# Running two experts chunk by chunk in turn, with the last pair staggered by three chunks

## The chip, the cores and the metric

The kernel is one program on one core of a Trainium2 chip. The metric is the device time of one execution in microseconds. The five engines have their own instruction streams, each executed in the order in which the program issues it: TensorE (PE, with its weight loads PEld), VectorE (DVE), ScalarE (ACT), GpSimd (POOL) and SyncE (SP, which here only issues loads).

## The reference

The reference is a two-layer decoder trunk on 256 tokens of width 1024. The change lies in the second layer's channel mixer, eight SwiGLU experts of which each token uses two:

```python
logits = (t @ router_w).astype(jnp.float32)
top_v, top_i = lax.top_k(logits, TOP_K)          # TOP_K = 2 of N_EXPERTS = 8
top_w = jax.nn.softmax(top_v, axis=-1)
gates = jnp.sum(jax.nn.one_hot(top_i, N_EXPERTS) * top_w[..., None], axis=1)
for e in range(N_EXPERTS):
    y = y + gates[:, e:e + 1] * swiglu(t, w_gate[e], w_up[e], w_down[e])
# swiglu(h, g, u, d) = (silu(h @ g) * (h @ u)) @ d, with d_ff = 3584
```

After it come a gated residual add and a final RMSNorm of each row.

## The kernel before

**The weight stream.** Every weight is float32 and is split on the chip into a high part (fp32r) and a rest. The class `Stream` does this for all weights in the order in which they are used. SP loads units of 1 MB (128 x 2048 floats) into raw buffers (line 144), ACT copies a unit to its high part `whi` (line 162), DVE subtracts to get the rest `wlo` (line 183). In the expert part there are four places for `whi` and three for `wlo`. When TensorE's program asks for unit n (`get`), the program issues `whi` of unit n+3 and `wlo` of unit n+2. Both overwrite the place of unit n-1, so they wait until TensorE has finished with that unit.

**One turn.** Each of the eight experts is cut into CH = 7 chunks of 512 hidden columns. A chunk has six units: two for gate, two for up, two for down. The program works in turns, one chunk each, with the down products one turn late. A turn for chunk (e, ch) issues, in this order:

- the gate products of the chunk into `ps_gate` (`wide`, line 1099), with the transposes of the previous chunk's activation in their middle (`turn`, line 1137, then ACT and DVE split it into `g`, lines 446 and 447)
- the up products into `ps_up` (also `wide`), with ACT's Silu of the gate bank in their middle (line 1262)
- the down products of the previous chunk, `pend`, into two banks `ps_y` (`down`, line 1159), and among them DVE's product `act * ps_up` (`product`, line 1280).

So a turn takes its gate and up products from its own chunk, and its down products from the chunk of the turn before.

**Wide and narrow experts.** Up to 128 tokens are gathered per expert. If an expert has more than 64, each pair of weight blocks needs three passes (high x high, high x rest, rest x high). If it has at most 64, the high and the low parts of its tokens stand side by side in the 128 columns and two passes do, but the two halves of the result have to be added afterwards: ACT copies the bank (`folded`, line 1111) and one product with `onto` adds it (line 951). The choice is made when the program runs. `by_width(e, wide, narrow, *sums)` writes both versions and a branch of TensorE's sequencer picks one (line 947). In a turn whose `pend` is of the same expert, the addition onto `ps_up` rides inside the narrow side of a down step's branch; otherwise it has a branch of its own, whose other side is empty (lines 1277 and 1278). With the inputs of this run experts 0, 2, 3 and 6 are wide, and 1, 4, 5 and 7 are narrow: a turn of a wide expert has 24 gate products, one of a narrow expert 16.

**Order of the experts.** They run one after another, 56 turns. The gathered tokens `xe` are made for two experts at a time, at the last turn of each odd expert. The gate and up banks come from four rotating banks "A", `ps_y` from two banks "C".

**Small work, one job a step.** A deque `jobs` gives up one entry at each `step()`. A turn has 15 steps: 7 in the gate products, 4 in the up products, 4 in the down products. When an expert is through, `finish(e)` queues seven entries (two copies `y_fold` line 1175, nothing, an addition under a branch, line 1180, nothing, then twice `y_out` line 1186 with its DMA to `y_rows` in DRAM, line 1187). Expert 7's result never goes to DRAM. For the others `bring_back` queues 22 entries after turn (7,2): four indirect gathers of `y_rows` by POOL (`gather_rows`, line 1196), six empty ones, and then four times ACT's `second` (line 1200), DVE's `first` (line 1203) and DVE's `onto_x` (lines 1207 and 1208). `second` and `first` need the gathered rows.

**The end.** After the last turn the last chunk's down products and `last_rows` follow: the scatter of expert 7's rows, the final norm and the stores.

Of the kernel before, what the change touches and what calls it, by code (L numbers as in the profile page):

```python
# [14 lines left out]
F32 = mybir.dt.float32  # L15
# [4 lines left out]
AF = mybir.ActivationFunctionType  # L20
# [3 lines left out]
P = 128  # L24
D = 1024
KD = D // P
# [7 lines left out]
E = 8  # L34
CH = 7
FC = FF // CH
NFC = FC // P
# [5 lines left out]
CAP = P  # L43

NARROW = 64


V_ADAB, V_ATTN, V_FFN, V_QN, V_KVN, V_OUT, V_FB = 0, 48, 56, 64, 66, 67, 75
# [193 lines left out]
def trunk_kernel(ctx: ExitStack, tc: tile.TileContext, x, c, positions, w_early, w_moe, router_w,  # L242
                 vecs, ada_b, final_g, consts, out):
    nc = tc.nc
# [16 lines left out]
    def bank(tag, shape, name):  # L261
        return psum.tile(shape, F32, tag=tag, name=name, bufs={"A": 4, "B": 2, "C": 2}[tag])
# [105 lines left out]
    order = early_order()  # L368
# [530 lines left out]
    def experts(l, outer, dram, ps_x, rs):  # L899
# [17 lines left out]
        w = outer.tile([P, 4, NB], F32, name="w")  # L917
# [26 lines left out]
        def by_width(e, wide, narrow, *more):  # L944


            with tc.If((held[0] & (1 << e)) == 0) as cmp:
                wide()
            with cmp.Else():
                for steps in (*more, narrow):  # L950
                    steps()  # L951

        held = []
# [26 lines left out]
        with tc.tile_pool(name="route", bufs=1, reuse_waits="tile") as pool:  # L980
# [9 lines left out]
            for c in halves:  # L990
                for b in range(NB):
                    ps = bank("B" if c.start else "A", [P, 512], "ps_h")
# [4 lines left out]
            ps = bank("A", [P, NB, P], "ps_r")  # L997
# [36 lines left out]
            picked = pick(0)  # L1034
            pk = next(picked)
# [34 lines left out]
        with tc.tile_pool(name="moe", bufs=1, reuse_waits="tile") as pool:  # L1070
# [36 lines left out]
            def folded(ps):  # L1107


                t = pool.tile([P, FC], F32R, name="fold")  # L1110
                nc.scalar.activation(t, ps, AF.Copy)  # L1111
                return partial(nc.tensor.matmul, ps, onto, t, start=False, stop=True, skip_group_check=True)

            y_ps, jobs = {}, deque()

            def step():

                job = jobs.popleft() if jobs else None
                if job is not None:
                    job()  # L1120
# [20 lines left out]
                    g += [both[:, i].rearrange("p w s -> p (w s)") for i in range(n)]  # L1141
                    yield

            def down(pend, *sums):
                e, ch, g = pend
                if ch == 0:
                    y_ps[e] = [bank("C", [P, 512], "ps_y") for _ in range(2)]
                for f in range(NFC):
                    hi, lo = ws.half()
                    both = g[f]  # L1150

                    def products(*passes):
                        first, last = ch == 0 and f == 0, ch == CH - 1 and f == NFC - 1
                        steps = [(n, hf) for n in range(len(passes)) for hf in range(2)]
                        if last:
                            steps.sort(key=lambda s: s[1])
                        for n, hf in steps:
                            part, w = passes[n]
                            nc.tensor.matmul(y_ps[e][hf], both[:, part], w[:, halves[hf]], start=(first and n == 0),  # L1159
                                             stop=(last and n == len(passes) - 1))  # L1160

                    first, second, even = slice(0, CAP), slice(CAP, 2 * CAP), slice(0, 2 * CAP, 2)
                    by_width(e, partial(products, (first, hi), (first, lo), (second, hi)),
                             partial(products, (even, hi), (even, lo)), *(sums if f == 1 else ()))
                    yield f
                    step()

# [45 lines left out]
            def last_rows(e, fg):  # L1213

                o = out.rearrange("(b p) d -> p b d", p=P)
                bt = back.pop(e)
                ts = [scratch([P, 512], F32, "yt") for _ in range(2)]
                for hf, c in enumerate(halves):
                    nc.vector.tensor_mul(ts[hf], y_ps[e][hf], rows[l, 5][:, c])
                rs = []  # L1220
                for b in range(NB):
                    ss = tiny.tile([P, 2], F32, name="ss", bufs=4)
                    for hf, c in enumerate(halves):
                        ps = bank("A", [P, 512], "ps_sc")
                        nc.tensor.matmul(ps, bt[:, b * P:(b + 1) * P], ts[hf], start=True, stop=True)  # L1225
                        xs = x_sb[:, b, c]
                        nc.vector.scalar_tensor_tensor(xs, ps, gates[:, b, e:e + 1], xs, ALU.mult, ALU.add)
                        square_sum(xs, ss[:, hf:hf + 1])
                    rs.append(row_r(ss, D, "x"))
                for b in range(NB):  # L1230
                    for c in halves:
                        t = scratch([P, 512], F32, "fin")
                        nc.vector.scalar_tensor_tensor(t, x_sb[:, b, c], rs[b], fg[:, c], ALU.mult, ALU.mult)  # L1233
                        nc.sync.dma_start(o[:, b, c], t)

            pend = None
# [3 lines left out]
            held.append(nc.tensor.value_load(bits[0:1, 0:1], min_val=0, max_val=(1 << E) - 1))  # L1240
            next(picked)
            jobs += [None, None, None, None] + puts + [gating, rows_and_shares]
            for e in range(E):
                for ch in range(CH):
                    pg = bank("A", [P, FC], "ps_gate")
                    for k in wide(e, pg):
                        if (e, ch) == (0, 0) and k % 2:
                            next(ahead, None)
                        elif k == 5 and pend is not None:
                            pend, *_ = turn(pend)  # L1250
                        else:
                            step()
                    add = folded(pg)
                    act = pool.tile([P, FC], F32, name="act")
                    if ch == CH - 2 and e % 2 and e + 1 < E:
                        picked = pick(e + 1)
                        next(picked)
                    pu = bank("A", [P, FC], "ps_up")
                    ahead = gather(e + 1, pk) if ch == CH - 1 and e % 2 and e + 1 < E else iter(())
                    for k in wide(e, pu, add):  # L1260
                        if k == 4:
                            nc.scalar.activation(act, pg, AF.Silu)
                            if (e, ch) == (E - 1, CH - 1):
                                nc.scalar.preload_act_table_set("natural_log_exp_and_others")  # L1264
                        if k % 2:
                            next(ahead, None)
                        else:
                            step()
                    parts = deque([slice(0, FC)])
                    add = folded(pu)  # L1270

                    within = pend is not None and pend[0] == e and (e, ch) != (E - 1, CH - 1)

                    def product():
                        if parts:
                            if not within:
                                with tc.If((held[0] & (1 << e)) != 0):  # L1277
                                    add()
                            c = parts.popleft()
                            nc.vector.tensor_mul(act[:, c], act[:, c], pu[:, c])  # L1280

                    new, turned_ = (e, ch, act), iter(())
                    if (e, ch) == (E - 1, CH - 1):
                        turned_ = turn(new)
                        new = next(turned_)
                        product()
                        product()
                    for f in down(pend, *((add,) if within else ())) if pend is not None else ():
                        if f >= 2:
                            next(turned_, None)  # L1290
                        if f % 2:
                            product()
                    while parts:
                        product()
                    if ch == 0 and e:
                        jobs.extend(finish(e - 1))
                    if (e, ch) == (E - 1, 2):
                        jobs.extend(bring_back())
                    if ch == CH - 2 and e % 2 and e + 1 < E:
                        pk = next(picked)  # L1300
                    pend = new
                while jobs:
                    step()
            for _ in turned_:
                pass
            fg = raw_pool.tile([P, RAW], F32, tag="raw", name="fg")[:, :D]
            nc.sync.dma_start(fg, bass.AP(tensor=final_g.tensor, offset=final_g.offset, ap=[[0, P], [1, D]]))
            for _ in down(pend):
                pass
            return last_rows(E - 1, fg)  # L1310

# [175 lines left out]
    return [w[i:i + 2] for w in (g, u, d) for i in range(0, len(w), 2)]  # L1487


def moe_order():  # L1490
    order, prev = [], []
    for e in range(E):
        for ch in range(CH):
            order += [(w, e, ch, k) for w in "gu" for k in range(KD // 2)] + prev
            prev = [("d", e, ch, f) for f in range(NFC)]
    return order + prev


# [109 lines left out]
```

## Time and profile before

| | |
|---|---|
| Median of 3 runs | 1466.74 us (1466.71 to 1466.99) |
| The profiled execution | 1467.24 us, span 1465.5 us |
| Granted TensorE clock, mean | 0.993 |
| PE / DVE / ACT busy over the span | 1381.7 / 1239.7 / 1058.2 us |
| Expert turns | 536.63 us to the end of the span |

The span runs from the first to the last instruction; the execution's time has 1.7 us around it. The useful way to read this kernel is by turns: each begins with the first gate product after a down product, and the busy time of each engine within a turn shows which of them is the limit there.

### The profile page before, as it was taken

To read this page: it belongs to the slowest core of one execution; us is meant where nothing else is said; L and a number is where in the kernel's file an instruction comes from. 1 tells how busy PE (TensorE), PEld (TensorE's weight loads), DVE (VectorE), ACT (ScalarE), POOL (GpSimd) and SP (SyncE) were. 2 spreads that over 40 slices of the span, in tenths; PEclk is the share of its full clock that TensorE was granted. 3 is DMA by queue.
4 is the path that set the end of the run, shared out by engine and by line. 5 is a ranking of instruction groups with operands and counts; after the bars stand their busy time and mean duration, and the time that the engine had idled before them with its cause. 6 is when DMAs were issued, how large, how long until landed. Compare 5 with 4: busy or idle time off the path is not lost. (4 is left out here: it accounts for less than half of the span.)

```text
span 1465.5 us, 21366 instructions
## 1 busy us (share of the span) xinstructions
PE 1381.7 (94%) x7305; PEld 1149.6 (78%) x7305; DVE 1239.7 (85%) x1177; ACT 1058.2 (72%) x1191; POOL 31.0 (2%) x42
## 2 busy tenths in 40 slices
PE   7999999999999989998999999999898999999876
PEld 7987899999899877886667887887666667887654
DVE  5987877777796469889988888888999998889997
ACT  5566644444557567778888778778989888778975
POOL 1000000000000020000000000000000000000200
PEclk9999999999999999999999999999999999999999
DMA  9974678787664229999999999999999999999993
GB/s 370 417 294 185 240 267 314 287 311 286 230 247 161 87 96 349 366 376 417 424 400 377 375 377 376 371 371 348 405 425 424 427 426 404 373 378 395 404 409 132
DMA packets 71100, 488.07 MB, mean 333 GB/s; under 512 B 8241, under 2 KB 8881, under 8 KB 13362
## 3 DMA queue, kind: packets, MB, share of 16 engines
q1 hardware_dynamic: 68178, 480.33, 83.6%
q10 hardware_dynamic: 2016, 3.67, 0.7%
q8 instruction: 96, 1.57, 0.4%
q0 software_dynamic: 768, 2.15, 0.4%
q14 instruction: 42, 0.34, 0.1%
HBM read 481.35 MB, written 4.72 MB: 332 GB/s over the span
## 5 line engine op out<-in xcount | busy, mean ns | idle before, releaser
L183 DVE TENSOR_TENSOR wlo<-raw,whi 128x2048 fp32r<-128x2048 f32 (+1 forms) x474 | 920.4, 1975 | 53.6 <-ACT whi L162 48.4
L162 ACT ACTIVATE whi<-raw 128x2048 fp32r<-128x2048 f32 (+1 forms) x474 | 764.5, 1662 | 106.9 <-PE ps_gu L396 77.4
L1099 PE MATMUL ps_gate<-whi,xe 128*128 128x512 f32 x672 | 243.6, 402 | 2.8 <-PEq L1180 2.2
L1099 PE MATMUL ps_up<-whi,xe 128*128 128x512 f32 x672 | 231.7, 391 | 0.0
L1099 PE MATMUL ps_gate<-wlo,xe 128*128 128x512 f32 x448 | 182.6, 408 | 24.4 <-DVE wlo L183 22.8
L1159 PE MATMUL ps_y<-whi,g 128*128 128x512 f32 x664 | 195.3, 393 | 1.6 <-PEq L1277 1.5
L1099 PE MATMUL ps_up<-wlo,xe 128*128 128x512 f32 x448 | 178.5, 398 | 13.8 <-DVE wlo L183 13.7
L1099 PEld LDWEIGHTS ps_gate<-whi,xe 128*128 128x128 f32 x672 | 128.5, 191 | 27.6 <-issue 4.4
L1159 PE MATMUL ps_y<-wlo,g 128*128 128x512 f32 x440 | 142.7, 403 | 5.9 <-DVE wlo L183 5.9
L1159 PEld LDWEIGHTS ps_y<-whi,g 128*128 128x128 f32 x664 | 125.9, 191 | 28.5 <-issue 2.9
L1099 PEld LDWEIGHTS ps_up<-whi,xe 128*128 128x128 f32 x672 | 127.7, 190 | 24.5
L1099 PEld LDWEIGHTS ps_gate<-wlo,xe 128*128 128x128 f32 x448 | 86.4, 193 | 59.9 <-DVE wlo L183 46.8
L395 PE MATMUL ps_gu<-dT_hi,whi 128*128 128x256 f32 x432 | 122.5, 284 | 0.0
L397 PE MATMUL ps_gu<-dT_hi,wlo 128*128 128x256 f32 x432 | 122.2, 283 | 0.0
L396 PE MATMUL ps_gu<-dT_lo,whi 128*128 128x256 f32 x432 | 122.2, 283 | 0.0
L1099 PEld LDWEIGHTS ps_up<-wlo,xe 128*128 128x128 f32 x448 | 85.6, 191 | 40.8 <-DVE wlo L183 24.1
L1159 PEld LDWEIGHTS ps_y<-wlo,g 128*128 128x128 f32 x440 | 80.7, 192 | 32.7 <-DVE wlo L183 19.2
L446 ACT ACTIVATE g<-ps_gt 128x512 fp32r<-128x512 f32 x55 | 32.9, 599 | 83.0 <-PE ps_gt L1137 83.0
L395 PEld LDWEIGHTS ps_gu<-dT_hi,whi 128*128 128x128 f32 x432 | 82.8, 192 | 1.2 <-issue 0.2
L396 PEld LDWEIGHTS ps_gu<-dT_lo,whi 128*128 128x128 f32 x432 | 82.8, 192 | 1.2 <-issue 0.2
L397 PEld LDWEIGHTS ps_gu<-dT_hi,wlo 128*128 128x128 f32 x432 | 82.8, 192 | 0.0
L330 DVE CUSTOM_DVE_ANT_0 raw<-raw,c_row,vc 128x1024 f32<-128x1024 f32 x56 | 71.1, 1279 | 0.0
(325 smaller groups left out, 1788.6 us busy)
## 6 DMA issues: line engine op xcount, KB each, us to landing
raw<-in_w_moe_dram SPq DMA_DIRECT2D x336, 1024.0 KB, 7.8
raw<-in_w_early_dram SPq DMA_DIRECT2D x114, 1024.0 KB, 7.0
y_rows<-y_out ACTq DMA_DIRECT2D x14, 256.0 KB, 8.7
raw<-in_w_early_dram SPq DMA_DIRECT2D x6, 512.0 KB, 8.6
gate<-in_ada_b_dram SPq DMA_DIRECT2D x4, 512.0 KB, 5.7
x_sb<-in_x_dram SPq DMA_DIRECT2D x1, 1024.0 KB, 7.1
out_dram<-fin SPq DMA_DIRECT2D x4, 256.0 KB, 2.0
fg<-in_final_g_dram SPq DMA_DIRECT2D x1, 512.0 KB, 6.8
```

The costliest lines, as they stand in the source:

```text
L162: self.nc.scalar.activation(hi, raw, AF.Copy)
L183: self.nc.vector.tensor_sub(parts[1], raw, parts[0].bitcast(F32))
L330: nc.vector.tensor_tensor_reduce(out=w, in0=w, in1=c_row, scale=1.0, scalar=vec(l, V_ADAB + section * KD + k, 1), op0=ALU.mult, op1=ALU.ad ...
L395: nc.tensor.matmul(out_, lh, rh, start=start, stop=False)
L396: nc.tensor.matmul(out_, lh, rl, start=False, stop=False)
L397: nc.tensor.matmul(out_, ll, rh, start=False, stop=stop)
L446: nc.scalar.activation(hi, src, AF.Copy)
L1099: nc.tensor.matmul(ps, both[:, part], w[:, halves[kk % 2]], start=(k == 0 and n == 1), stop=(k == KD - 2 and n == 2 * len(passes)))
L1159: nc.tensor.matmul(y_ps[e][hf], both[:, part], w[:, halves[hf]], start=(first and n == 0), stop=(last and n == len(passes) - 1))
```

## The change

The turns of two experts, 2i and 2i+1, alternate chunk by chunk. For the pair 6 and 7 a list `SKEW` gives the order 6 7 6 6 7 6 6 7 6 6 7 7 7 7, so that expert 6 has its last turn when expert 7 has three of its seven, and its last down products fall into the turn of 7's fourth. The weights are streamed in that order.

Each expert of a pair has two `ps_y` banks of its own, two "C" and two "A"; the other two "A" banks are one fixed `ps_gate` and one fixed `ps_up`. The chunk whose down products run in a turn is now mostly the other expert's. The addition onto `ps_up` rides inside the down step in all turns but the first and the last, and where the two experts differ it does so by a branch inside each side of the outer branch. `finish` is queued after the turn that holds an expert's last down products, and for expert 6 `bring_back` right behind it.

```diff
+SKEW = (0, 1, 0, 0, 1, 0, 0, 1, 0, 0, 1, 1, 1, 1)
...
+            pg, pu, *y_of = [bank("A", [P, 512], name) for name in ("ps_gate", "ps_up", "ps_yb", "ps_yb")]
+            y_of = [[bank("C", [P, 512], "ps_ya") for _ in range(2)], y_of]
...
-            def down(pend, *sums):
+            def down(pend, of, *sums):
...
-                    y_ps[e] = [bank("C", [P, 512], "ps_y") for _ in range(2)]
+                    y_ps[e] = y_of[e % 2]
...
-                    by_width(e, partial(products, (first, hi), (first, lo), (second, hi)),
-                             partial(products, (even, hi), (even, lo)), *(sums if f == 1 else ()))
+                    steps = (partial(products, (first, hi), (first, lo), (second, hi)),
+                             partial(products, (even, hi), (even, lo)))
+                    if f == 1 and sums and of != e:
+
+                        steps = [partial(by_width, of, x, x, *sums) for x in steps]
+                    by_width(e, *steps, *(sums if f == 1 and of == e else ()))
...
-            for e in range(E):
-                for ch in range(CH):
-                    pg = bank("A", [P, FC], "ps_gate")
...
+            for e, ch in moe_turns():
...
-                    within = pend is not None and pend[0] == e and (e, ch) != (E - 1, CH - 1)
...
+                within = pend is not None and not end
...
-                    if ch == 0 and e:
-                        jobs.extend(finish(e - 1))
-                    if (e, ch) == (E - 1, 2):
+                if pend is not None and pend[1] == CH - 1:
+                    jobs.extend(finish(pend[0]))
+                    if pend[0] == E - 2:
                         jobs.extend(bring_back())
...
+def moe_turns():
+
+
+    turns = [(e + i, ch) for e in range(0, E - 2, 2) for ch in range(CH) for i in range(2)]
+    ch = [0, 0]
+    for i in SKEW:
+        turns.append((E - 2 + i, ch[i]))
+        ch[i] += 1
+    return turns
```

## Rows read from the trace of the kernel before

**Rows 1.** The page, busy time of each engine over the whole span.
```profile
PE 1381.7 (94%) x7305; PEld 1149.6 (78%) x7305; DVE 1239.7 (85%) x1177; ACT 1058.2 (72%) x1191; POOL 31.0 (2%) x42
```

**Rows 2.** Timeline of PE at the borders of turn (7,0).
```profile
1334.57 0.62 PE L1159 MATMUL ps_y<-whi,g 128*128 128x512 f32 x2
1335.02 0.39 PE L1099 MATMUL ps_gate<-whi,xe 128*128 128x512 f32 x1
1335.26 0.39 PE L1099 MATMUL ps_gate<-wlo,xe 128*128 128x512 f32 x1
1335.49 0.39 PE L1099 MATMUL ps_gate<-whi,xe 128*128 128x512 f32 x1
...
1349.60 0.40 PE L1099 MATMUL ps_gate<-whi,xe 128*128 128x512 f32 x1
```

**Rows 3.** Windows cut at turn borders: PE, PEld, DVE, ACT, POOL, clock, DMA, GB/s.
```profile
550.89:569.39 18.50, 17.22 (x76) 13.93 (x77) 17.19 (x21) 14.35 (x12) 0.00 (x0) 1.00 0.86 324
569.39:653.42 84.03, 84.03 (x381) 69.54 (x380) 73.46 (x41) 65.53 (x51) 0.00 (x0) 1.00 0.98 371
653.42:668.00 14.58, 14.24 (x64) 11.34 (x62) 13.71 (x8) 13.37 (x11) 0.00 (x0) 1.00 1.00 400
761.30:778.08 16.78, 15.69 (x69) 12.35 (x68) 14.98 (x9) 13.54 (x12) 0.00 (x0) 1.00 0.94 343
1034.92:1107.04 72.12, 65.51 (x272) 48.11 (x270) 72.12 (x41) 64.96 (x51) 0.00 (x0) 1.00 1.01 421
1335.02:1349.60 14.58, 14.24 (x64) 11.34 (x62) 13.71 (x8) 13.37 (x11) 0.00 (x0) 1.00 1.00 410
1349.60:1365.21 15.61, 13.25 (x56) 9.65 (x54) 13.79 (x9) 13.40 (x14) 0.00 (x0) 1.00 1.00 399
1394.61:1418.05 23.44, 16.21 (x56) 11.71 (x54) 23.12 (x19) 16.20 (x15) 0.00 (x0) 0.85 1.00 404
```

**Rows 4.** Timeline of DVE over a turn of narrow expert 4.
```profile
1047.69 0.68 DVE L1280 TENSOR_TENSOR act<-act,ps_up 128x512 f32<-128x512 f32 x1
1048.28 6.69 DVE L183 TENSOR_TENSOR wlo<-raw,whi 128x2048 fp32r<-128x2048 f32 x3
1054.90 0.69 DVE L447 TENSOR_TENSOR g<-ps_gt,g 128x512 fp32r<-128x512 f32 x1
1055.51 6.69 DVE L183 TENSOR_TENSOR wlo<-raw,whi 128x2048 fp32r<-128x2048 f32 x3
1062.11 0.68 DVE L1280 TENSOR_TENSOR act<-act,ps_up 128x512 f32<-128x512 f32 x1
```

**Rows 5.** Timeline of DVE over a turn of wide expert 0.
```profile
633.25 0.69 DVE L1280 TENSOR_TENSOR act<-act,ps_up 128x512 f32<-128x512 f32 x1 [0.33 <-PE ps_y L1159]
633.86 6.70 DVE L183 TENSOR_TENSOR wlo<-raw,whi 128x2048 fp32r<-128x2048 f32 x3
641.96 0.69 DVE L447 TENSOR_TENSOR g<-ps_gt,g 128x512 fp32r<-128x512 f32 x1 [1.40 <-ACT g L446]
```

**Rows 6.** Waits from 536 us on: who waited for whom, us in total, times, longest.
```profile
PE ps_y L1159 <- PEq L1277: 1.5, 3, 0.6
...
ACT whi L162 <- DMA raw<-in_w_moe_dram: 0.8, 2, 0.5
```

**Rows 7.** Branches of line 947: duration in ns, smallest, median, largest.
```profile
L947 PEldq COMPARE_BRANCH  x1093: 66/176/372, 536.4 to 1453.0; - x183
```

**Rows 8.** Timeline of ACT: expert 6's rows leave in turn (7,1), the first `second`.
```profile
1355.71 0.60 ACT L1186 ACTIVATE y_out<-ps_y 128x512 f32<-128x512 f32 x1 [0.40 <-ACT y_out L1186]
1356.34 0.33 ACTq L1187 DMA_DIRECT2D y_rows<-y_out  x1
...
1360.81 0.59 ACT L1262 ACTIVATE act<-ps_gate 128x512 f32<-128x512 f32 x1
...
1390.16 0.72 ACT L1200 ACTIVATE got<-got,share 128x512 f32<-128x512 f32 x1
```

**Rows 9.** Timeline of POOL: the four gathers.
```profile
1366.76 2.85 POOL L1196 DMA_INDIRECT got<-y_rows,row_of  x1 [830.71 <-DVE wlo L183]
1369.92 1.75 POOL L1196 DMA_INDIRECT got<-y_rows,row_of  x1 [0.30 <-PE ps_gate L1099]
```

**Rows 10.** Tile `got`, the gathers' landing; then DMA issues, us from issue to landing.
```profile
DMA to landing us min/median/max: 10.5/13.4/15.0
...
y_rows<-y_out ACTq DMA_DIRECT2D x14, 256.0 KB, 8.7
...
gate<-in_ada_b_dram SPq DMA_DIRECT2D x4, 512.0 KB, 5.7
```

**Rows 11.** Timeline of DVE around the start of turn (7,2), then the first `first`.
```profile
1364.16 6.69 DVE L183 TENSOR_TENSOR wlo<-raw,whi 128x2048 fp32r<-128x2048 f32 x3
1370.78 0.69 DVE L447 TENSOR_TENSOR g<-ps_gt,g 128x512 fp32r<-128x512 f32 x1
...
1392.43 0.74 DVE L1203 SCALAR_TENSOR_TENSOR got<-got,share 128x512 f32<-128x512 f32 x1
```

More of the change, by code (lines that the diff above doesn't have):

```diff
@@ L1220, in last_rows @@
                 rs = []
+                free = [pg, pu, *y_of[E % 2]]
                 for b in range(NB):
@@ L1223, in last_rows @@
                     for hf, c in enumerate(halves):
-                        ps = bank("A", [P, 512], "ps_sc")
+                        ps = free.pop(0)
                         nc.tensor.matmul(ps, bt[:, b * P:(b + 1) * P], ts[hf], start=True, stop=True)
@@ L1242, in experts @@
             jobs += [None, None, None, None] + puts + [gating, rows_and_shares]
-            for e in range(E):
-                for ch in range(CH):
-                    pg = bank("A", [P, FC], "ps_gate")
[L1246 to L1270, printed above, removed]
-                    within = pend is not None and pend[0] == e and (e, ch) != (E - 1, CH - 1)
[L1274 to L1285, printed above, removed]
-                        product()
[L1287 to L1294, printed above, removed]
-                    if ch == 0 and e:
-                        jobs.extend(finish(e - 1))
-                    if (e, ch) == (E - 1, 2):
-                        jobs.extend(bring_back())
[L1299 to L1303, printed above, removed]
@@ new lines, in experts, with product @@
+            for e, ch in moe_turns():
+                end = (e, ch) == (E - 1, CH - 1)
+                for k in wide(e, pg):
+                    if (e, ch) == (0, 0) and k % 2:
+                        next(ahead, None)
+                    elif k == 5 and pend is not None:
+                        pend, *_ = turn(pend)
+                    else:
+                        step()
+                add = folded(pg)
+                act = pool.tile([P, FC], F32, name="act")
+                if ch == CH - 2 and e % 2 and e + 1 < E:
+                    picked = pick(e + 1)
+                    next(picked)
+                ahead = gather(e + 1, pk) if ch == CH - 1 and e % 2 and e + 1 < E else iter(())
+                for k in wide(e, pu, add):
+                    if k == 4:
+                        nc.scalar.activation(act, pg, AF.Silu)
+                        if end:
+                            nc.scalar.preload_act_table_set("natural_log_exp_and_others")
+                    if k % 2:
+                        next(ahead, None)
+                    else:
+                        step()
+                parts = deque([slice(0, FC)])
+                add = folded(pu)
+                within = pend is not None and not end
+                def product():
+                    if parts:
+                        if not within:
+                            with tc.If((held[0] & (1 << e)) != 0):
+                                add()
+                        c = parts.popleft()
+                        nc.vector.tensor_mul(act[:, c], act[:, c], pu[:, c])
+                new, turned_ = (e, ch, act), iter(())
+                if end:
+                    turned_ = turn(new)
+                    new = next(turned_)
+                    product()
+                    product()
+                for f in down(pend, e, *((add,) if within else ())) if pend is not None else ():
+                    if f >= 2:
+                        next(turned_, None)
+                    if f % 2:
+                        product()
+                while parts:
+                    product()
+                if pend is not None and pend[1] == CH - 1:
+                    jobs.extend(finish(pend[0]))
+                    if pend[0] == E - 2:
+                        jobs.extend(bring_back())
+                if ch == CH - 2 and e % 2 and e + 1 < E:
+                    pk = next(picked)
+                pend = new
@@ L1304, in experts @@
+            while jobs:
+                step()
             for _ in turned_:
@@ L1307, in experts @@
             nc.sync.dma_start(fg, bass.AP(tensor=final_g.tensor, offset=final_g.offset, ap=[[0, P], [1, D]]))
-            for _ in down(pend):
+            for _ in down(pend, E - 1):
                 pass
@@ L1487, in moe_units @@
     return [w[i:i + 2] for w in (g, u, d) for i in range(0, len(w), 2)]
+def moe_turns():
[5 more added lines that the diff above has]
+    return turns
 def moe_order():
     order, prev = [], []
[L1492 to L1495, printed above, removed]
+    for e, ch in moe_turns():
+        order += [(w, e, ch, k) for w in "gu" for k in range(KD // 2)] + prev
+        prev = [("d", e, ch, f) for f in range(NFC)]
     return order + prev
```

## The prediction

> **What bounds the kernel now.** I read the page first, then the borders of the turns, then the engines' busy time between borders, then the DVE stream inside a turn, and last the path of expert 6's rows. Over the whole span PE is busy 94% and DVE 85% [rows 1]; that is an average over stages and says little here. Turn borders are found on PE's timeline: turn (7,0) runs from 1335.02 to 1349.60, and inside it the products start 0.23 us apart [rows 2].
>
> I call a turn by the width of its gate and up products and then of its down products: WW, WN, NW, NN. Cut at the borders [rows 3], the expert part shows two limits. Five WW turns take 84.03 us, 16.81 each, and PE is busy in all of it. Five NN turns take 72.12 us, 14.42 each, and now DVE is busy in all of it while PE has 65.51. Two NW turns, (1,0) and (7,0), each right after a WW turn, take 14.58. The DVE stream says why 14.42 is a floor [rows 4]: three `wlo` of 1 MB units, `g`, three more `wlo`, the product, with no idle time, 1047.69 to 1062.11. That work is the same for a wide expert, only that DVE there stands between its pieces, 1.40 us before `g` for instance [rows 5]. So PE waits for DVE in narrow experts and DVE for PE in wide ones. Loads are not the limit: in the whole expert part ACT waited 0.8 us for raw weights [rows 6], and five NN turns ran at 421 GB/s [rows 3].
>
> **The change part by part, the turns.** Alternating puts WN and NW turns where WW and NN turns were, but only where a wide expert meets a narrow one: pairs 0/1 and 6/7. Pair 2/3 is wide twice and 4/5 narrow twice, so their turns stay WW and NN: nothing.
>
> NW is measured, 14.58. An undisturbed WN turn is not in the trace. It has 8 products fewer than WW, so 16.81 - 8 x 0.23 = 14.97; below, DVE's 14.42 bounds it, above, the 16.78 of turn (2,0), which is WN with the branch of line 1277 and leftovers of the gathering in it [rows 3]. I take 14.97, because PE is the limit in the WW turn that it is derived from. A WW and an NN turn, 31.23, so become a WN and an NW turn, 29.55: 1.68 saved. The floor, two DVE turns, would save 2.39; the upper end, 16.78 + 14.58, would lose 0.13.
>
> Pair 0/1 has six WW and six NN turns to convert: 6 x 1.68 = 10.1 us. In pair 6/7 the order 6 6 7 leaves a WW turn in each group of three, and the last three turns of expert 7 stay NN: three conversions, 5.0 us. Ends for the nine: -21.5 and +1.2 us.
>
> Start: the second turn, now (1,0), still carries DVE work left from routing. DVE had 17.19 us in it, and the turn took 18.50 as WW [rows 3], 1.7 over a plain one. As NW it cannot be shorter than 17.2, 2.6 over. Cost 0.9.
>
> **Branches and banks.** The addition onto `ps_up` loses its own branch. PE waited for that three times, 1.5 us in total [rows 6]; all three are in turns that lose it: -1.5. In its place comes a branch inside a branch. The existing branches take 0.176 us in the median and 0.372 at most [rows 7], on a sequencer that issues ahead of PE, and five WW turns with 13 of them each show PE without a gap [rows 3]. I take 0 (worse: third rival).
>
> One bank each for gate and up instead of rotating ones: the product that frees `ps_up` ends at 1048.4 [rows 4], before the next turn's first gate product at 1049.3, and the up products come 16 products later. The Silu that reads the gate bank is over at 1361.4 [rows 8], 3.8 us before the next turn. Cost 0. Without that cover PE would wait for the rest of a 0.7 us product.
>
> `finish` made an NN turn 15.61 instead of 14.42 [rows 3], 1.2 us. It runs seven times before and after: 0. If the second pair of y banks spares half of each, -4; a loss I exclude, its instructions are the same.
>
> **The rows of expert 6.** The work of `bring_back` costs (7,4) 23.44 - 14.42 = 9.0 us, because DVE is full there [rows 3]. It falls into an NN turn again, (7,5): no difference. What differs is how long it has been prepared. Before, `finish(6)` ran in (7,1) and the first `second` stood in ACT's stream at 1390.16 [rows 8], 23.4 us after the first gather began [rows 9]. Now expert 6 is through in the turn of (7,3), `finish` fills the gate products of (7,4), and the gathers, two empty steps short of `second`, come right behind.
>
> Put the start of (7,4) at T and use (7,1), which began at 1349.60, as its pattern:
>
> - The second DMA to `y_rows` is issued at 1356.34, T + 6.7 [rows 8].
> - POOL begins the first gather at 1366.76, when that DMA has landed, T + 17.2, and the second at 1369.92, T + 20.3 [rows 9]. `second` reads what the second gather brings.
> - A gather lands 10.5 to 15.0 us after its issue, 13.4 in the median [rows 10]: T + 30.8 to T + 33.7 with the first two.
> - Turn (7,5) begins at T + 15.6. `second` is its third step, `first` its fourth, both before the program asks for the second gate unit. DVE by then has the `wlo` of three units to do, which in (7,2) were done at 1370.85, 5.6 us into the turn [rows 11]: T + 21.2.
>
> From then on `first` heads DVE's queue and waits for `second`, and behind it stand all further `wlo`, behind these PE. With 0.72 us for `second` DVE stands from T + 21.2 to between T + 31.5 and T + 34.4: 10.3 to 13.2 us, in a stage where DVE is the limit, so all of it is lost. ACT stands too, so no `whi` is made ahead.
>
> The lower end: as soon as DVE stands no raw buffer is freed and the weight stream dries up, so the gather may finish faster. A 512 KB load took 5.7 us elsewhere [rows 10]; with that, 5.5 us are lost. Most of the gather still runs under the stream, so I take 10.5. PE idle that long will drop to the lower of its two clock levels, as (7,4) did before with 0.85 granted; DVE was busy 23.12 of those 23.44 us [rows 3], so this adds nothing.
>
> **Sum.** -10.1 - 5.0 + 0.9 - 1.5 + 10.5 = -5.2 us. Against the profiled execution, 1467.24 (span 1465.5 and 1.7 around it), that is 1462.0. The median of the runs is 0.5 below that execution, so I forecast 1461.5.
>
> **Rivals.**
>
> *The gathers are hardly late.* If puts and gathers land sooner than in (7,1), or the stream dries up early, 0 to 5.5 us are lost instead of 10.5: 1451 to 1456.5. For it: 5.7 us for a load of the same size. Against: every gather took over 10 us, and the puts 8.7 in the median [rows 10]. The Trainium skill ("DMA: Bandwidth & Descriptors", section "Anatomy of one DMA — SWDGE (gpsimd) path") puts a DMA at about 2.0 us plus its bytes at 436 GB/s. As an estimate from that page a put would take 2.6 and a gather 3.2 us, the second gather would land before T + 21.2, and the sum would be -15.7. The trace does not agree: 13.4 us in the median, with the weight stream on the same engines.
>
> *The lead is too short (slower).* DVE can be two units ahead of PE at most. In a WW turn it idles 16.81 - 14.42 = 2.4 us because it waits at `g` and at the product for PE. If in a WN turn it still idles that much, the turn takes 16.8, nothing is saved in the nine conversions, and the time is 1461.5 + 15.1 = 1476.6. It decides against the change from 2.9 + 5.2 = 8 us lost, that is 0.9 us in each of nine. For it: (2,0), 16.78. Against: NW turns with 14.58, where DVE was the one that ran through.
>
> *The inner branch drains PE (slower).* With an addition in one side only, the skipped side must still signal, and line 1277 shows what that costs when nothing else is in it: 1.5 us in three, 0.5 each [rows 6]. A turn whose own expert is wide and whose down products are the other's has such a side: 6 + 7 + 7 + 4 = 24 turns, nearly all bound by PE, 12 us: 1473.5. Against: an inner side still holds the down products, which can carry the signal, as the outer ones do now. The Trainium skill ("Runtime: NRT & Kernel Launch", section "Instruction fetch mechanics") says that a taken branch whose target lies outside the fetched window stalls for a fetch, and the doubled code makes turns longer. No branch among 1093 took over 0.372 us here.
>
> **How the numbers follow.** Forecast 0.50 (1457 to 1465, mostly the landing time); gathers hardly late 0.27; lead too short 0.10; drains 0.10; the rest 0.03. A measurement of this kernel can tell about 0.2%, 2.9 us, from no change: faster is below 1463.8, slower above 1469.7. Of the forecast four fifths lie below 1463.8; with the first rival 0.68. The rest of it and mild forms of the two slow rivals make 0.12, the slow rivals 0.20. The range of 1449 to 1471 holds the forecast, nearly all of the first rival and mild forms of the others; the likeliest one's own is 1457 to 1465.
>
> **What the profile after would show.** WN turns near 15.0 and NW turns near 14.6 in pairs 0/1 and 6/7, unchanged steady turns in 2/3 and 4/5; no wait of PE on line 1277 in expert turns except the first and last. In (7,5) ACT idle at line 1200 for a DMA of `got`, and DVE idle about 10 us at line 1203. I am wrong if that idle time is missing, if WN turns stay above 15.9, or if PE waits for its sequencer at line 947 or a new one like it in wide turns.

## The result, and the profile after

The changed kernel takes 1480.39 us (median of 4 runs, 1475.68 to 1480.68) against 1466.72; the ratio is 1.0087, 95% interval 1.0066 to 1.0108. It is slower by 13.7 us. The forecast was 1461.5 with a range up to 1471: wrong in direction and outside its range.

The profiled execution has a span of 1478.9, 13.4 over the one before. I found the borders of the turns as before and cut windows there; the columns are those of [rows 3].

```profile
552.40:571.05 18.65, 16.25 (x62) 12.45 (x63) 17.02 (x19) 14.59 (x12) 0.00 (x0) 0.91 0.85 315
664.79:679.90 15.11, 15.11 (x69) 12.49 (x68) 12.95 (x8) 10.94 (x10) 0.00 (x0) 1.00 0.99 406
679.90:696.06 16.16, 14.85 (x64) 11.13 (x62) 16.16 (x10) 15.13 (x12) 0.00 (x0) 1.00 1.00 398
815.83:832.65 16.82, 16.82 (x78) 13.91 (x77) 14.70 (x9) 13.11 (x11) 0.00 (x0) 1.00 0.98 382
1266.19:1284.23 18.04, 17.13 (x78) 13.84 (x76) 16.40 (x10) 14.82 (x12) 0.00 (x0) 1.00 0.98 383
1284.23:1298.85 14.62, 14.28 (x64) 11.26 (x63) 14.50 (x9) 13.41 (x11) 0.00 (x0) 1.00 0.99 405
1298.85:1313.93 15.08, 15.08 (x70) 12.49 (x68) 12.97 (x8) 10.97 (x10) 0.00 (x0) 1.00 1.01 419
1394.29:1409.57 15.28, 13.01 (x55) 9.65 (x54) 12.94 (x8) 13.40 (x14) 0.00 (x0) 1.00 1.00 409
1409.57:1442.74 33.17, 15.92 (x56) 11.05 (x54) 21.23 (x19) 17.46 (x16) 5.53 (x4) 0.82 0.78 289
1442.74:1478.90 36.16, 25.19 (x83) 16.66 (x81) 27.22 (x26) 17.12 (x24) 0.00 (x0) 0.83 0.17 65
```

The rows are turn (1,0); a WN and an NW turn of pair 0/1; a WW turn of pair 2/3; a WW, NW and WN turn of pair 6/7; then (7,4), (7,5), and (7,6) with the end. Two things stand out. In pair 0/1 a WN turn takes 15.11, as forecast, but the NW turn after it takes 16.16 and DVE is busy in all of it: together 31.27, no less than the 31.23 of a WW and an NN turn. And (7,5) takes 33.17.

Here is DVE in that WN turn and at the start of the NW turn, which begins at 679.90 (timeline after):

```profile
670.14 0.69 DVE L449 TENSOR_TENSOR g<-ps_gt,g 128x512 fp32r<-128x512 f32 x1 [1.43 <-ACT g L448]
670.75 2.28 DVE L185 TENSOR_TENSOR wlo<-raw,whi 128x2048 fp32r<-128x2048 f32 x1
673.40 4.49 DVE L185 TENSOR_TENSOR wlo<-raw,whi 128x2048 fp32r<-128x2048 f32 x2 [0.37 <-ACT whi L164]
677.82 0.68 DVE L1289 TENSOR_TENSOR act<-act,ps_up 128x512 f32<-128x512 f32 x1
678.86 6.70 DVE L185 TENSOR_TENSOR wlo<-raw,whi 128x2048 fp32r<-128x2048 f32 x3 [0.37 <-ACT whi L164]
```

DVE idles 1.43, 0.37 and 0.37 us; the first, at `g`, is the wait that a WW turn shows [rows 5]. It has nothing more to do by the program's order, and then has no stock when the light turn begins.

The end of the stall in (7,5), on PE, ACT and DVE (three timelines after):

```profile
1415.21 0.40 PE L1101 MATMUL ps_up<-whi,xe 128*128 128x512 f32 x1
1427.79 0.79 PE L1101 MATMUL ps_up<-wlo,xe 128*128 128x512 f32 x1 [12.19 <-DVE wlo L185]
```
```profile
1400.67 0.33 ACTq L1197 DMA_DIRECT2D y_rows<-y_out  x1
...
1424.03 0.72 ACT L1210 ACTIVATE got<-got,share 128x512 f32<-128x512 f32 x1 [12.41 <-DMA got<-y_rows,row_of]
```
```profile
1408.49 4.49 DVE L185 TENSOR_TENSOR wlo<-raw,whi 128x2048 fp32r<-128x2048 f32 x2
1424.78 0.75 DVE L1213 SCALAR_TENSOR_TENSOR got<-got,share 128x512 f32<-128x512 f32 x1 [11.80 <-ACT got L1210]
```

This is the chain that was forecast: `first` heads DVE's queue for 11.80 us because `second` waits for a gather. DVE had two units done when it began to stand, not three, and PE stopped after the first `whi` product of the first up unit.

**A correction to the section on the kernel.** It says that the program, asked for unit n, issues `whi` of n+3 and `wlo` of n+2. These rows show one unit less: with PE in the gate products of (7,5), DVE had done the two gate units and no up unit. The condition in `pump` holds one place back: `whi` is issued up to n+2 and `wlo` up to n+1. They overwrite the places of unit n-2, not n-1: the third place for `wlo` and the fourth for `whi` do not lengthen the lead.

### The profile page after: what moved, and what is told of

Its sections match the earlier page's. It is cut to its first block, busy times and chain, and to the rows that moved or that the text cites. A ratio compares the mean times of both kernels' runs of the same rounds, so it can differ in the third digit from the quotient of the medians.

```text
span 1478.9 us, 21453 instructions
## 1 busy us (share of the span) xinstructions
PE 1387.3 (94%) x7305; PEld 1155.4 (78%) x7305; DVE 1239.6 (84%) x1177; ACT 1057.7 (72%) x1191; POOL 27.6 (2%) x42
## 5 line engine op out<-in xcount | busy, mean ns | idle before, releaser
L1165 PE MATMUL ps_ya<-whi,g 128*128 128x512 f32 x392 | 113.7, 391 | 0.0
L1165 PEld LDWEIGHTS ps_ya<-whi,g 128*128 128x128 f32 x392 | 73.7, 189 | 14.8
L1165 PE MATMUL ps_yb<-whi,g 128*128 128x512 f32 x272 | 83.7, 399 | 0.2
L1165 PE MATMUL ps_yb<-wlo,g 128*128 128x512 f32 x216 | 70.8, 407 | 5.5 <-DVE wlo L185 5.5
L1165 PE MATMUL ps_ya<-wlo,g 128*128 128x512 f32 x224 | 71.9, 399 | 3.1 <-DVE wlo L185 3.1
```

## The experiments

Each time is a median, with the ratio to the kernel before on the same chip; that kernel had 1467.15, 1467.37, 1468.45 and 1467.51 us in the four groups.

**x_skew: the gathers in time.** The changed kernel with

```diff
-SKEW = (0, 1, 0, 0, 1, 0, 0, 1, 0, 0, 1, 1, 1, 1)
+SKEW = (0, 0, 1, 0, 0, 1, 0, 0, 0, 1, 1, 1, 1, 1)
...
-                return ([partial(gather_rows, j, b) for b in range(NB) for j in range(2)] + [None] * 6 +
+                return ([partial(gather_rows, j, b) for b in range(NB) for j in range(2)] + [None] * 24 +
```

> Expert 6 is run four chunks ahead instead of three (order 6 6 7 6 6 7 6 6 6 7 7 7 7 7) and 18 more empty steps stand between the gathers and the first `second`, so that the gathered rows are there when ACT and DVE come to them. Theory: the late gathers cost the changed kernel about 12 us in turn (7,5) and nothing else in the last turns; ACT's wait for the DMA of `got` and DVE's behind it vanish, and the time falls by 10 to 13 us to 1468 to 1470, about the time of the kernel before, because the alternation itself gains nothing. Rival: the alternation itself loses time, by branches or single banks, and the stall was partly hidden; then it falls by less than 6 us and stays above 1474.

1462.68 us, ratio 0.9971 (0.9958 to 0.9983). Nobody waits for the gathers any more. It fell by 17.7, more than the theory's 13, to 4.5 below the kernel before. The last four turns of the profiled execution, which took 1465.32:

```profile
1378.64:1393.89 15.25, 12.98 (x55) 9.71 (x54) 12.85 (x8) 13.30 (x14) 0.00 (x0) 1.00 0.99 402
1393.89:1408.34 14.45, 13.14 (x56) 9.62 (x54) 14.45 (x9) 13.00 (x11) 8.72 (x4) 1.00 0.99 407
1408.34:1426.88 18.54, 13.43 (x55) 9.65 (x54) 18.44 (x16) 17.38 (x16) 0.00 (x0) 1.00 1.01 422
1426.88:1463.50 36.62, 22.62 (x83) 14.28 (x81) 29.91 (x29) 17.12 (x24) 0.00 (x0) 0.97 0.31 125
```

From the `finish` turn on that is 84.86 us with one plain NN turn more; without it 70.41, against 84.61 in the changed kernel. So by this comparison the late gathers cost 14.2 us, 2.4 more than DVE's idle time. But 1.4 of the 2.4 is not theirs. It is DVE's wait for the up products in the last turn, here in the changed kernel, in `x_skew` and in the kernel before:

```profile
1457.26 0.69 DVE L1289 TENSOR_TENSOR act<-act,ps_up 128x512 f32<-128x512 f32 x1 [2.53 <-PE ps_up L1287]
1442.75 0.69 DVE L1289 TENSOR_TENSOR act<-act,ps_up 128x512 f32<-128x512 f32 x1 [1.12 <-PE ps_up L1287]
1444.54 0.69 DVE L1280 TENSOR_TENSOR act<-act,ps_up 128x512 f32<-128x512 f32 x1 [2.52 <-PE ps_up L1278]
```

The kernel before has the same wait without late gathers. In `x_skew` it is shorter, and there more of the jobs of `bring_back` run in the last turn, ahead of it. A further 0.8 is DVE's wait for `xe` at the end, 0.92 against 0.15. So the late gathers cost between 11.8 and 12.8 us.

**early: the same stall in the old order.** The kernel before, with `bring_back` queued right behind `finish(6)`:

```diff
                     if ch == 0 and e:
                         jobs.extend(finish(e - 1))
-                    if (e, ch) == (E - 1, 2):
-                        jobs.extend(bring_back())
+                        if e == E - 1:
+                            jobs.extend(bring_back())
```

> The kernel before with one change: `bring_back` is queued right behind `finish(6)` instead of after turn (7,2), so that in this old order too the first `second` comes two turns after expert 6 ends. Theory: ACT waits for the second gather and DVE behind it, 11 to 13 us, and the time is 1477 to 1480; the loss belongs to the place of `bring_back` and not to the alternation. Rival: with seven chunks of one narrow expert to go the lost time is made up, or the gathers are late only because of the alternating stream; then it is below 1471.

1480.14 us, ratio 1.0088 (1.0071 to 1.0105), at the upper end of the theory's range. The waits on tile `got` are those of the changed kernel, 12.4 us of ACT and 11.8 us of DVE:

```profile
  ACT got L1200: 12.4, 1
  DVE got L1203: 11.8, 1
```

The order of the experts was not touched. From the first turn of expert 6 to the end the profiled execution took 261.64 us, against 249.67 before: 12.0 more. The loss belongs to the place of `bring_back`, and the four narrow turns behind it did not make it up, since DVE is the limit there.

**banks_only: the code without the order.** The changed kernel, with the experts one after another and 29 empty steps before `second`, so that it stands where it stood before:

```diff
-SKEW = (0, 1, 0, 0, 1, 0, 0, 1, 0, 0, 1, 1, 1, 1)
+SKEW = (0, 0, 0, 0, 0, 0, 0, 1, 1, 1, 1, 1, 1, 1)
...
-    turns = [(e + i, ch) for e in range(0, E - 2, 2) for ch in range(CH) for i in range(2)]
+    turns = [(e, ch) for e in range(E - 2) for ch in range(CH)]
```

> The changed kernel's code, with its fixed gate and up banks, its four y banks and the addition inside the down step, but the experts one after another as before, and `bring_back` with as many empty steps before it as before. Theory: neither banks nor branches cost anything, and the three waits at the old branch are gone: 1463 to 1467, the same as before or 1 to 3 us less. Rival: the code costs a part of the change's 13.7 us; then it is above 1469.

1465.99 us, ratio 0.9992 (0.9983 to 1.0001). Fixed banks cost nothing that can be measured. In this order the branch within a branch comes only in the seven turns where two experts meet. It is tested by the changed kernel's WW turns of pair 2/3 above, which all have it: 16.82 with PE busy throughout, as before.

**seq67: pair 0/1 alternating, 6 and 7 in sequence.** Only the last pair's order is set back, again with 29 empty steps:

```diff
-SKEW = (0, 1, 0, 0, 1, 0, 0, 1, 0, 0, 1, 1, 1, 1)
+SKEW = (0, 0, 0, 0, 0, 0, 0, 1, 1, 1, 1, 1, 1, 1)
```

> The changed kernel with pairs 0/1, 2/3 and 4/5 alternating as in it, but expert 7 wholly after expert 6, and `bring_back` with as many empty steps as before. Theory: with one unit of lead a WN and an NW turn, 15.1 and 16.1, take as long as a WW and an NN turn, so pair 0/1 stays at 224 to 226 us and the time at 1463 to 1468. Rival: the alternation of pair 0/1 is what cost the time; then it is above 1471.

1466.61 us, ratio 0.9991 (0.9982 to 1.0001). Pair 0/1 took 223.88 us, against 224.05 in `banks_only`, the same code in sequence. As the theory says: with this lead the alternation neither gains nor loses in pair 0/1.

**lead: one unit more of lead.** The changed kernel with

```diff
-            ahead = len(self.turns) - (self.prepped >= self.given + need)
+            ahead = len(self.turns) - (self.hold and self.prepped >= self.given + need)
```

where `hold` is true up to the experts and false from there on. `whi` is then issued up to unit n+3 and `wlo` up to n+2, in the places that exist.

> The changed kernel, but in the expert part the stream issues each `whi` and `wlo` one unit earlier: `wlo` of unit n+2 instead of n+1 when unit n is asked for, with the places that are already there. Theory: a turn that is narrow above gains nothing after a WN turn because DVE has only one unit of lead; with two, NW turns in pair 0/1 fall from 16.1 to about 14.6 us with WN turns near 15.1, nine conversions bring 1.5 us each, and the time falls by 12 to 16 us to 1464 to 1468 (the wait for the gathers stays). Rival: something else keeps DVE back (ACT's order, `g`, the product, the single banks); then NW turns stay above 15.8 and the time above 1477.

1456.19 us, ratio 0.9923 (0.9906 to 0.9939), 24.2 below the changed kernel. That is more than the theory's 12 to 16; `lead_before` below shows a part of the reason. Its WN and NW turn in pair 0/1, and WW, NW and WN in pair 6/7:

```profile
656.56:671.67 15.11, 15.11 (x70) 12.49 (x69) 14.58 (x9) 12.61 (x10) 0.00 (x0) 1.00 1.01 422
671.67:686.08 14.41, 14.31 (x64) 11.35 (x63) 14.41 (x9) 13.60 (x11) 0.00 (x0) 1.00 1.01 425
1297.09:1313.91 16.82, 16.82 (x77) 13.91 (x76) 16.20 (x9) 14.07 (x11) 0.00 (x0) 1.00 1.01 407
1313.91:1328.04 14.13, 14.13 (x64) 11.43 (x63) 13.87 (x8) 13.14 (x10) 0.00 (x0) 1.00 1.02 413
1328.04:1343.12 15.08, 15.08 (x70) 12.49 (x68) 13.88 (x9) 12.60 (x10) 0.00 (x0) 1.00 1.01 415
```

In the WN turn DVE now works 14.58 of 15.11 us instead of 12.95, and the NW turn is 14.41 instead of 16.16. The two turns take 29.52. The wait for the gathers is still in this run.

**lead_low and lead_hi: `wlo` alone, `whi` alone.** Both use the same `hold`. The first leaves the condition and issues every `wlo` whose `whi` has been issued:

```diff
-        self.rest(n)
+        self.rest(n if self.hold else None)
```

The second is `lead` with one `wlo` held back:

```diff
-                self.rest(len(self.ready))
+                self.rest(len(self.ready) - (not self.hold))
```

What was expected of `wlo` alone:

> The changed kernel; only `wlo` is issued one unit earlier (unit n+2 when n is asked for), `whi` stays at unit n+2. Theory: it is DVE's lead over PE that the alternation lacks, and `wlo` has a third place that is not used for it; NW turns of pair 0/1 fall from 16.1 to 14.4 to 14.9 us and the time to 1456 to 1462. Rival: it is ACT's lead that helped (a `whi` made in the same step comes too late for DVE); then NW turns stay above 15.5 and the time above 1472.

1484.79 us, ratio 1.0122 (1.0107 to 1.0138): the theory is wrong, and both signs of the rival are there. The NW turn is 16.71 with DVE busy 16.63:

```profile
664.98:680.07 15.09, 15.09 (x70) 12.50 (x68) 12.51 (x7) 11.02 (x10) 0.00 (x0) 1.00 1.00 410
680.07:696.78 16.71, 14.68 (x64) 11.10 (x62) 16.63 (x11) 15.10 (x12) 0.00 (x0) 1.00 0.98 393
```

DVE now stands at `wlo` and waits for `whi`. From 600 to 720 us that is 10.4 us in this run (first row) and 2.9 us in the changed kernel (second):

```profile
DVE wlo L186 <- ACT whi L165: 10.4, 8, 1.7
```
```profile
DVE wlo L185 <- ACT whi L164: 2.9, 8, 0.4
```

And of `whi` alone:

> The changed kernel; only `whi` is issued one unit earlier (unit n+3 when n is asked for), `wlo` stays at unit n+1. With the run that moved `wlo` alone and the one that moved both this completes the four cases. Theory: both are needed, because a `wlo` of unit n+2 can only run ahead if its `whi` is there, and a `whi` alone gives DVE nothing to do: NW turns of pair 0/1 stay at 15.8 to 16.3 us and the time at 1474 to 1482. Rival: ACT's lead is what counts; then NW turns fall below 15 and the time below 1465.

1474.31 us, ratio 1.0047 (1.0029 to 1.0065), in the theory's range at its lower end, but the NW turn lies below the theory's 15.8. The NW and WN turns, 15.64 and 15.08, make 30.72, a third of the way to 29.52:

```profile
643.86:659.50 15.64, 14.85 (x64) 11.10 (x62) 15.57 (x10) 13.95 (x11) 0.00 (x0) 1.00 1.01 419
659.50:674.58 15.08, 15.08 (x69) 12.49 (x68) 13.51 (x8) 12.60 (x10) 0.00 (x0) 1.00 1.00 409
```

So the lead is one of two engines in series: `whi` alone gives a part, `wlo` alone costs, and only both together give the whole.

**lead_before: the old order with that lead.** The same edit in the kernel before.

> The kernel before with the same one unit more of lead. Theory: WW turns are bound by PE and NN turns by DVE, so lead alone changes nothing in them: 16.8 and 14.4 as before; only turns with extra work (`finish`, the first ones) may gain, and the time falls by 0 to 4 us, 1463 to 1467. Rival: the lead speeds up the stream as such, whatever the order of experts; then it falls by more than 8 us, and the gain of the changed kernel with more lead says nothing on alternation.

1454.69 us, ratio 0.9915 (0.9899 to 0.9932), 12.5 less. The theory's 0 to 4 us is wrong. The time is the rival's, its reason is not: steady WW and NN turns stay, but the stretches where the limit passes from PE to DVE get shorter. The rows are turn (0,6), which stays, and (1,0), then (1,2) to (1,4):

```profile
635.36:652.16 16.80, 16.80 (x78) 13.91 (x77) 14.96 (x8) 13.46 (x10) 0.00 (x0) 1.00 0.93 363
652.16:665.98 13.82, 13.82 (x63) 11.49 (x62) 13.57 (x8) 13.03 (x10) 0.00 (x0) 1.00 1.01 414
...
681.68:694.58 12.90, 12.46 (x55) 9.97 (x54) 12.90 (x8) 12.90 (x11) 0.00 (x0) 1.00 1.00 407
694.58:708.37 13.79, 12.75 (x56) 9.67 (x54) 13.79 (x9) 13.05 (x11) 0.00 (x0) 1.00 1.01 426
708.37:722.79 14.42, 13.02 (x56) 9.62 (x54) 14.42 (x9) 13.12 (x11) 0.00 (x0) 1.00 1.01 426
```

The NW turn is 13.82 instead of 14.58, and two NN turns lie below 14.42, until the stock of finished units is used up. As the rival warned, the gain of `lead` over the changed kernel is not all alternation.

**lead_skew: lead and gathers in time.** Both edits in the changed kernel.

> Both corrections at once: the unit more of lead, and expert 6 four chunks ahead with 18 more empty steps before the first `second`. Theory: lead and stall are separate losses, so their gains add, 24 us and 17 us off the changed kernel's 1480, less some 2 us because a unit more is ready when the stall begins: 1440 to 1445, and 10 to 14 us below the kernel before with the same lead (1454.7), which is what the alternation brings once DVE has two units. Rival: the lead already gave what alternation can give, since DVE's work is the sum that counts; then it is 1452 to 1456, no better than the old order with the lead.

1441.81 us, ratio 0.9829 (0.9815 to 0.9842): 25.6 below the kernel before and 38.6 below the changed one. Against the old order with the same lead it is 12.9 lower, within the theory's 10 to 14. Pair 0/1, which has neither late gathers nor a skew, shows it best, here in `lead` and in `lead_before`:

```profile
537.85:751.13 213.28, 209.32 (x940) 169.44 (x939) 202.03 (x128) 187.95 (x151) 0.00 (x0) 1.00 0.99 408
536.40:758.16 221.76, 209.90 (x939) 168.50 (x939) 203.09 (x128) 191.47 (x155) 0.00 (x0) 1.00 0.98 389
```

With two units of lead on both sides the alternation saves 8.5 us in this pair, of which the new code alone may be 0.6 (224.05 in `banks_only`, 224.67 before); with one unit it saved nothing.

**warm and warm2: the clock in the stall.** 48 products of the identity with itself in turn (7,5) of the changed kernel, added work whose results nothing uses; in `warm` between the first and the second up unit, in `warm2` between the gate and the up products. The edit of `warm2`:

```diff
+                if (e, ch) == (E - 1, CH - 2):
+                    for _ in range(48):
+                        nc.tensor.matmul(y_of[0][0][:, :P], ident, ident, start=True, stop=True)
```

> The changed kernel with 48 products of the identity with itself into a y bank that is free by then, in turn (7,5) between the first and the second up unit, where PE waits for the late gathers; they add work and no result uses them. DVE is idle 11.8 us there, but expert 7's last turns lose some 14 against the version whose gathers are in time, and the granted clock is 0.82 in the turn and 0.83 in the next. Theory: the 2 to 3 us that DVE's idle time doesn't explain are PE at the lower clock level; with PE busy in most of the wait the clock stays above 0.9 in both turns and the time falls by 2 to 3 us to 1477 to 1479. Rival: the lower clock is covered by DVE; then the clock rises and the time stays within 1 us of 1480 or grows.

1484.23 us, ratio 1.0117 (1.0098 to 1.0135). The run did not test it: PE stood one unit earlier, so the products came after the wait.

> As the run before, but the 48 products stand between the gate and the up products of turn (7,5): the trace of that run shows PE's wait at the first up unit, one unit earlier than assumed there, so its products ran after the wait and only added 6 to 10 us of work. Now they run within the wait of about 12 us. Theory: the 2 to 3 us that DVE's idle time doesn't explain are PE at the lower clock level; the clock stays above 0.9 in (7,5) and the next turn and the time falls by 2 to 3 us to 1477 to 1479. Rival: the lower clock is covered by DVE, and the time stays within 1 us of 1480.

1477.19 us, ratio 1.0077 (1.0059 to 1.0094). The last two turns:

```profile
1406.01:1437.58 31.57, 25.70 (x151) 21.54 (x150) 20.41 (x19) 16.82 (x16) 5.22 (x4) 0.95 0.77 299
1437.58:1474.20 36.62, 23.41 (x83) 15.43 (x81) 27.87 (x26) 17.64 (x25) 0.00 (x0) 0.93 0.18 71
```

The clock is 0.95 and 0.93 instead of 0.82 and 0.83, and the two turns take 68.19 instead of 69.33: 1.1 us. The rest of the median's 3.2 us lies elsewhere, since turn (7,5) began 3.6 us earlier here although the kernels are the same up to it. So the median decides neither way. Nor is the 1.1 all clock, for DVE's wait at `first` was shorter too, 11.02 instead of 11.80:

```profile
1420.43 0.75 DVE L1213 SCALAR_TENSOR_TENSOR got<-got,share 128x512 f32<-128x512 f32 x1 [11.02 <-ACT got L1210]
```

That is 0.8 of the 1.1. By these two profiles, one each, at most some 0.4 us is left for the lower clock, too little to be told from other differences between the two.

## Why the prediction was wrong

**The conversions: the step that failed.** The prediction took 16.81 - 8 x 0.23 for WN and the measured 14.58 for NW, and saved 1.68 nine times. WN was right, 15.08 to 15.11. What failed is the price of its neighbours, which were taken from other surroundings. In pair 0/1 it is NW: 14.58 had been measured after WW turns [rows 3] and was used after WN turns, where it came to 16.16. Six light units, the two down units of WN and the four gate and up units of NW, come there in one run. PE takes one in 1.84 us (8 products 0.23 us apart), DVE makes one in 2.23 (three in 6.69 [rows 4]), and one unit of lead does not bridge that. Pair 0/1 gave nothing instead of 10.1 us. In pair 6/7 NW follows WW and took 14.62, as priced; there the WW turn behind WN pays, 18.04 instead of 16.81. PE stands at its first gate unit, as in the WW turn that begins at 1313.93:

```profile
1315.23 0.50 PE L1101 MATMUL ps_gate<-wlo,xe 128*128 128x512 f32 x1 [0.91 <-DVE wlo L185]
```

So three turns WW, NW, WN took 18.04 + 14.62 + 15.08 = 47.74 against 2 x 16.81 + 14.42 = 48.04, 0.3 a group instead of 1.7. `seq67` and `lead` show both sides: nothing with one unit, 29.52 for the two turns with two, and the prediction's sum was 29.55. The sum was that of a stream with two units of lead, which the kernel does not have: a misread condition in `pump`.

**The rival of the short lead came true, with its loss in the other turn.** It had a chance of 0.10. It let DVE idle 2.4 us in WN and made WN 16.8; DVE does idle 2.2 us there, but the bill comes in the turn behind it. The price is nearly the same: 0.7 us is saved of 15.1. The test that was named, WN turns above 15.9, would have missed it.

**The rows of expert 6: the mechanism was right, the size nearly, in part by luck.** The order of events was as written. The second gather began at 1414.25 and its rows were in use at 1424.03, with T = 1394.29 that is T + 29.7 instead of T + 30.8 or later. DVE began to stand at T + 18.7 instead of T + 21.2, since it had one unit less to do, again by the lead. 10.5 was forecast and 11.80 was DVE's idle time: DVE stood 2.5 us sooner, and the gather was also there sooner, so two misses partly cancel. The price was 11.8 to 12.8, and 12.0 in `early`, which shows that it does not depend on the alternation. "This adds nothing" on the clock holds to within the 0.4 us of `warm2`.

**Branches, banks and `finish`.** Right within the measurement: `banks_only` 0.9992. The third rival, a drain at the inner branch, is out by the WW turns of pair 2/3 and the WN turns, where PE is busy throughout.

**The start.** (1,0) took 18.65, 4.1 over a plain NW turn, instead of 2.6; DVE had 17.02 in it as forecast, and the clock was 0.91.

**The Trainium skill's rule for DMA times** ("DMA: Bandwidth & Descriptors", section "Anatomy of one DMA — SWDGE (gpsimd) path", about 2.0 us plus bytes at 436 GB/s) gave 3.2 us for a gather as an estimate. The section is about DMAs that POOL issues, as the gathers are; the puts are ACT's. The measured 9.8 of the changed kernel (smallest and median of four) do not agree:

```profile
DMA to landing us min/median/max: 9.8/9.8/10.6
```

The DMA engines were not free: between 1413 and 1424 us they moved 406 GB/s.

**By numbers.** By stretches of the two profiled executions, the expert part began 1.2 us later, in a part that the change does not touch. Pair 0/1 took 225.71 instead of 224.67 us, where -9.2 was forecast. Pairs 2/3 and 4/5 took 452.45 instead of 454.53. Pair 6/7 with the end took 262.88 instead of 249.67, +13.2 where +5.5 was forecast. Together these are the 13.4 of the span. Of the 18.6 us between -5.2 and 13.4, the conversions are 14.4 (15.1 forecast, 0.7 measured), the stall 1.3 (10.5 and 11.8), the start 1.5 and the later beginning 1.2; the small rest was not taken apart. That the four runs of the changed kernel lie between 1475.68 and 1480.68 is not explained; the profiles of this kernel and of `warm2`, which are the same program up to (7,5), differ most in the first two turns, 33.2 against 31.2 us.

## What to carry to other kernels

Alternating work with two different limits averages them only if the lead carries the slower producer through the lighter work: here one unit did not and two did. Measure the lead in finished units on the timeline before pricing it, and read a turn's price in the context in which it will stand. Where a producer chain crosses two engines, as here, look at the lead of both. And whatever moves earlier in an in-order queue has to be checked against the slowest thing that it reads: the rows of expert 6 were in use 29.7 us after the start of the `finish` turn, and one turn and two steps were too little cover for that.

## What the runs showed of the hardware

I had not expected one unit of lead, in places that were already there, to take 12.5 us off the old order, where I had given it 0 to 4.

With PE idle some 12 us the granted clock fell to the lower of the two levels, 1.2 GHz, and was still there when PE began again:

```profile
1427.79:1430.00 2.21, 2.21 (x5) 1.82 (x6) 2.17 (x4) 2.21 (x3) 0.00 (x0) 0.50 0.58 111
```

It was 0.82 on average over (7,5) after, and 0.95 with 48 small products in the wait.

The gathers were quicker after, 9.8 us in the median against 13.4 [rows 10], while the DMA engines moved as much: 406 GB/s from 1413 to 1424 us after, 418 from 1370 to 1383 us before. What differs is the share of the queue with the weight loads, after and before:

```profile
q1 hardware_dynamic: 383, 2.74, 61.1%
q1 hardware_dynamic: 550, 3.98, 73.2%
```

That the gathers were quicker because of this smaller share is likely, but no run tests it.
